# Slots of three tile pools made 32 bytes longer, and two raw weight buffers in place of three, in a two-layer float32 decoder trunk

## The chip, the core and the metric

The kernel runs on one core of a Trainium2 chip. The metric is the device time of one execution in microseconds (us); lower is better. The engines are TensorE (PE: matrix products, with its weight loads shown apart as PEld), VectorE (DVE), ScalarE (ACT), GpSimd (POOL) and SyncE (SP, which here issues most DMA transfers). SBUF is the on-chip memory of 128 partitions; an address below is a byte offset within a partition, which is the same for all 128.

## The reference

A trunk of two layers over 1024 tokens with a width of 1024, in float32. Layer 0 mixes tokens with latent attention (8 heads), layer 1 with a gated spatial unit in chunks of 128 tokens. Each mixer is followed by a feed-forward block of width 4096 and by a gated per-layer embedding of width 256.

```python
def reference(x, p, positions, norm_mix, norm_ffn, norm_ple, ...):
    h = x
    for i in range(2):
        hn = rms_norm(h, norm_mix[i])
        h = h + (mla_mixer(hn, ...) if i % 2 == 0 else gmlp_mixer(hn, ...))
        hn = rms_norm(h, norm_ffn[i])
        h = h + jnp.square(jax.nn.relu(hn @ ffn_w_up[i])) @ ffn_w_down[i]
        hn = rms_norm(h, norm_ple[i])
        h = h + jax.nn.sigmoid(hn @ ple_w_gate[i]) * (p[i] @ ple_w_proj[i])
    return h

def gmlp_mixer(hn, w_in, ln_g, ln_b, w_s, b_s, w_out):
    u, v = jnp.split(jax.nn.gelu(hn @ w_in), 2, axis=-1)
    v = layer_norm(v, ln_g, ln_b)           # then in chunks of 128 tokens, 8 groups
    sv = jnp.einsum('gts,bnsgd->bntgd', w_s * mask, v) + b_s.T
    return (u * sv) @ w_out
```

## The kernel before

**Products.** Every operand of a product is split into a high and a low part (`split`, L106: ACT copies to the 4-byte type fp32r, DVE subtracts), and a product is three matmuls: high by high, high by low, low by high. A matmul has a stationary operand of 128x128, which its own weight load brings in, and a moving operand of mostly 512 columns. In `gemm` (L134) weights stand still and activations move; in the first product of the gated unit (`proj_mm`, tiles vp and up) it is the other way round. The output is feature-major: 128 rows by 1024 tokens in two chunks of 512.

**Pools.** The tile framework cuts SBUF into pools, each a row of equal slots that its tiles take in turn; a tile waits until the last reader of the slot's former tile is done. Those of the change:

- pa, tag a: 2 slots of 16 KB: hidden activations of the feed-forward (f_ah, f_al), the gated unit's y (yh, yl), heads 4 to 7 of the attention output (o4h, o4l), latents, gates (sig).
- pw, tag w: 6 slots of 4 KB: split weights (wh, wl, wb).
- phn, tag hn: 32 slots of 2 KB: the normed residual (n_00h, n_00l, and so on: feature tile, chunk, high or low part), and before that the attention output of heads 0 to 3 (oh, ol).
- pr, tag raw: 3 slots of 4 KB: unsplit weights (raw), x in layer 0's start (x), p (praw), parked values (vr).

All slot lengths are multiples of 512 bytes, so that all slots of a pool stand at one address modulo 512. In the built program this is 288 for the w and a slots and 320 for the hn slots.

**What is where.** Feed-forward up products (tiles f0u, f1u): moving hn (320), stationary w (288). Down products (f0d, f1d): moving a (288), stationary w (288). Output products: go moves a against w; wo moves hn in its first half, a in its second, against w. pg (the embedding's gate) moves hn against w. vp and up move weights (288) against stationary hn slices (320).

**Order.** `ffn` (L253) runs 8 slices s of 512 hidden features: up products, squared ReLU into f_ah and f_al, down products added to the residual h. Weight blocks of 512 KB are loaded by SP as slots come free (L114), so SP runs ahead by as many blocks as pr has slots. After the up products of slice 1, `p_split` (L311) loads p in two halves into raw slots, turns them with PE transposes (tile pp) and splits them into pth and ptl; then come the down products of slice 1. The last slice's down products go one token chunk at a time (`down_sweeps`, L294, tile names wb). Sums of squares for the norm are products with a tile of ones (onesr, L214). In layer 0's start `block_x` transposes one block of 128 tokens of x (tiles x, xp) at a time. The identity for transposes, idf, is made by POOL at the very start (L71). The order on each engine is set by a scheduler from the code's order and its own estimates.

Of the kernel before, what the change touches and what calls it, by code (L numbers as in the profile page):

```python
# [8 lines left out]
F32 = mybir.dt.float32  # L9
# [7 lines left out]
P = 128  # L17
T = 1024
# [21 lines left out]
def trunk(ctx: ExitStack, tc: tile.TileContext, I, out):  # L40
# [6 lines left out]
    pw = ctx.enter_context(tc.tile_pool(name="pw", bufs=6))  # L47
    pr = ctx.enter_context(tc.tile_pool(name="pr", bufs=3))
    pt = ctx.enter_context(tc.tile_pool(name="pt", bufs=4))
# [18 lines left out]

# [1 line left out]
    idf = const.tile([P, P], F32, name="idf")  # L70
# [28 lines left out]
    def gain(kind, layer):  # L99
        o = kind * 16 + layer * 8  # L100
        return [gT[:, o + k:o + k + 1] for k in range(KT)]

# [1 line left out]
    cnt = [0]  # L104
# [15 lines left out]
    def load_packed(w, k0, f0, nk, nf):  # L120
        """a block whose hi and lo share one slot"""
        cnt[0] += 1
        i = cnt[0]
        raw = pr.tile([P, nk, nf], F32, tag="raw", name=f"raw{i}")
        nc.sync.dma_start(raw, w[k0 * P:(k0 + nk) * P, f0:f0 + nf].rearrange("(k p) f -> p k f", p=P))
        both = pw.tile([P, 2, nk, nf], F32R, tag="w", name=f"wb{i}")
        split(both[:, 0], both[:, 1], raw)
        return both[:, 0], both[:, 1]

# [1 line left out]
    par = [0]  # L131
    CS = [slice(0, 512), slice(512, T)]

    def gemm(blocks, rhs, f, name, seq=False, only=None):  # L134
        """one 128-row output tile, over both token chunks or one; rhs[k][c] = (hi, lo).
        Returns (accumulator, columns) units."""
        if only is not None:
            acc = {only: pso(name)}
            units = [(acc[only], CS[only])]
            csets = [(only,)]  # L140
        else:
            par[0] ^= 1
            if par[0]:
                full = psg(name)
                acc = [full[:, CS[c]] for c in range(2)]
                units = [(full, slice(0, T))] if not seq else [(acc[c], CS[c]) for c in range(2)]
            else:
                acc = [pso(f"{name}_{c}") for c in range(2)]
                units = [(acc[c], CS[c]) for c in range(2)]
            csets = [(0,), (1,)] if seq else [(0, 1)]  # L150
        nk = len(rhs)
        w = [(hi[:, kk, f * P:(f + 1) * P], lo[:, kk, f * P:(f + 1) * P]) for hi, lo in blocks for kk in range(hi.shape[1])]
        for cset in csets:
            for k, (wh, wl) in enumerate(w):
                for c in cset:
                    mm(acc[c], wh, rhs[k][c][0], k == 0, False)
                for c in cset:
                    mm(acc[c], wh, rhs[k][c][1], False, False)
                for c in cset:
                    mm(acc[c], wl, rhs[k][c][0], False, k == nk - 1)  # L160
        return units
# [3 lines left out]

# [1 line left out]
    class Norm:  # L167
        """split of h * gain per (feature tile, token chunk); the scale per token is applied after the product"""

# [39 lines left out]
        def sums(self, c, st):  # L209
            """sum of squares of chunk c on every partition of st, an accumulator of 512 columns"""  # L210
            if c not in self.shl:
                self.halve(c)
            shl = self.shl[c]
            mm(st, onesr, shl[:, 0], True, False)  # L214
            mm(st, onesr, shl[:, 1], False, True)
            self.st[c] = st

        def roots(self, *chunks):
            """1/rms on every partition"""
            if self.rb is None:  # L220
                self.rb = pb.tile([P, T], F32, tag="rb", name=f"{self.name}_rb")
            with tc.issue_after(self.last.ins):
                table = S.preload_act_table_set(LNEXP)
            for c in chunks:
                rb, st = self.rb[:, CS[c]], self.st[c]
                with tc.issue_after(table.ins):
                    S.activation(rb, st, AF.Ln, bias=epst, scale=1.0 / D)
                vr = tmp(f"{self.name}{c}_vr", [P, 2, 512])
                v, rr = vr[:, 0], vr[:, 1]
                S.activation(v, st, AF.Identity, bias=epst, scale=1.0 / D)  # L230
                S.activation(rb, rb, AF.Exp, scale=-0.5)
                S.activation(rr, rb, AF.Square)
                V.scalar_tensor_tensor(v, v, -0.5, rr, op0=ALU.mult, op1=ALU.mult)
                V.scalar_tensor_tensor(rb, v, 1.5, rb, op0=ALU.add, op1=ALU.mult)
# [5 lines left out]
        def tokens(self, c, pp=None):  # L240
            """the scale per token, tokens on partitions"""
            if self.r is None:
                self.r = pb.tile([P, NB], F32, tag="rtok", name=f"{self.name}_r")
            if pp is None:
                pp = pso(f"{self.name}_tok{c}")
            for b in range(4):
                PE.transpose(pp[:, b * P:(b + 1) * P], self.rb[:, (c * 4 + b) * P:(c * 4 + b + 1) * P], idf)
            V.tensor_copy(self.r[:, c * 4:c * 4 + 4], pp.rearrange("p (b q) -> p b q", q=P)[:, :, 0])

# [1 line left out]
    halves = {}  # L251
# [42 lines left out]
    def down_sweeps(w, k0, rhs, h, name, nxt, late):  # L294
        """one token chunk after the other, so that the next product can start on the first"""
        for c in range(2):
# [12 lines left out]

# [1 line left out]
    def p_split(i):  # L311
        """p transposed and split: two k tiles of [128, T]"""
        pth = pb.tile([P, 2, T], F32R, tag="pth", name=f"pth{i}")
# [46 lines left out]

# [1 line left out]
    def load_cols(w, f0, name, slots):  # L362
        """columns of a [1024, F] weight as moving operand: per k tile (hi, lo), in the order of use"""
        nf = 256 if slots == "w" else 512
# [19 lines left out]
    def gmlp(h, nrm, nxt):  # L384
# [12 lines left out]
        def spatial_weights():  # L397
            # masked spatial weights, transposed and split; bias per position
            wr = pr.tile([P, 8, P], F32, tag="raw", name="wsraw")
# [30 lines left out]
        for cc, (_, f0, nf) in enumerate(plan):  # L430
# [28 lines left out]
            w = nw  # L459
# [3 lines left out]

        # layer norm statistics
        mv = const.tile([P, NB, 2], F32, name="mv")
# [64 lines left out]

# [1 line left out]
    def ple_out(i, h, nrm):  # L532
# [61 lines left out]

# [1 line left out]
    def mla(h, park):  # L596
        w_down, w_uq, w_ukv, w_out = (I[n][0] for n in ("mla_w_down", "mla_w_uq", "mla_w_ukv", "mla_w_out"))
        with tc.tile_pool(name="pm", bufs=1) as pm:
# [12 lines left out]
            def small_loads():  # L611
                """what the rotary tables and the later norms take"""
                pi = pm.tile([NB, P], I32, name="posi")
# [10 lines left out]
                return gb, pi, gq, inv  # L624
            # down projection weights, gains folded in
            xraw = {}
# [126 lines left out]
            def drain(*gens):  # L753
                """lets each generator run, the later ones three steps behind"""
                live = list(gens)
                n = 0
                while live:
                    for j, g in list(enumerate(gens)):
                        if g in live and n >= 3 * j and next(g, True):
                            live.remove(g)  # L760
                    n += 1
# [3 lines left out]
            def rotary_key(hf):  # L765
                """shared rotary key of half of the tokens: [hi; lo] stacked on partitions"""
                hb = slice(hf * 4, hf * 4 + 4)
# [17 lines left out]

            # per head
            kT, vt, qt, prob, O, proj, pts = ({} for _ in range(7))
# [7 lines left out]
            def q_weights(hp, part):  # L795
                """query weights of a pair of heads: k tiles 0 and 1, or 2"""
                n = 384
# [288 lines left out]
    def rsqrt_small(ss, eps, name):  # L1086
        """1/sqrt(ss + eps) on a small tile, one Newton step after the tables"""
        n = ss.shape[1]
# [10 lines left out]
    def wo_first(rhs, h):  # L1099
        """first half of the output projection, a step per next()"""  # L1100
        w = I["mla_w_out"][0]
# [9 lines left out]
    for _ in filler:  # L1111
        pass
    phn = ctx.enter_context(tc.tile_pool(name="phn", bufs=32))
    n1 = Norm("n1", gain(1, 0))
    rhs1 = []
# [49 lines left out]
```

## Time and profile before

| | before |
|---|---|
| times of the runs | 2746.99 and 2745.89 us, median 2746.44 |
| span of the profiled execution | 2745.7 us |
| TensorE busy | 2711.9 us (99%), 13600 matmuls |
| weight loads busy | 2285.2 us (83%), 13600 |
| VectorE, ScalarE, GpSimd busy | 45%, 33%, 12% |
| DMA traffic | 163.54 MB, mean 60 GB/s |

The profile is of one execution. Its own time is known by its span alone, from the first to the last instruction; the two timed runs lie 0.2 and 1.3 us above that span, which is what may lie around it. Matmuls overlap in a pipeline, so the duration of one (some 390 ns) is no price; the price is the distance from one start to the next, called the pitch below.

### The profile page before, as it was taken

Reading aid. Unit: us, or ns where it says so; the run is one execution under the profiler, and the core shown is the slowest. Engines: PE = TensorE matmul, PEld = TensorE weight load, DVE = VectorE, ACT = ScalarE, POOL = GpSimd, SP = SyncE. Lnnn points to the kernel's source line nnn. Section 1 sums busy time; section 2 is a strip of 40 time slices with the busy share of each in tenths; the row PEclk is TensorE's granted clock in tenths of the full one; section 3 lists DMA queues with packets and bytes.
Section 4 is the critical chain, followed back from the end, with each engine's and each line's share of the span. In section 5 each row is a group of like instructions: output and inputs, shape, how many; then the busy total and the mean of one; then the engine's idle time right before and its main releaser. Section 6 shows DMA issues by size and latency. Waiting matters only on the chain.

```text
span 2745.7 us, 33465 instructions
## 1 busy us (share of the span) xinstructions
PE 2711.9 (99%) x13600; PEld 2285.2 (83%) x13600; DVE 1230.3 (45%) x1964; ACT 905.3 (33%) x1815; POOL 318.9 (12%) x459
## 2 busy tenths in 40 slices
PE   8999999999999999999999999999999999999999
PEld 8999888888888888887888788888888888888899
DVE  5777774533333333375522534436433333333652
ACT  4677772411221122164422312215221122211541
POOL 4444330000000000001211332120000000000000
PEclk9999999999999999999999999999999999999999
DMA  5100012112111111132332312211121111111221
GB/s 164 54 18 6 23 55 69 47 47 65 50 46 47 46 53 48 34 99 75 100 104 94 94 40 84 85 46 54 49 65 40 51 49 47 54 46 39 68 90 35
DMA packets 151209, 163.54 MB, mean 60 GB/s; under 512 B 6496, under 2 KB 133024, under 8 KB 151056
## 3 DMA queue, kind: packets, MB, share of 16 engines
q1 hardware_dynamic: 146240, 146.31, 17.0%
q0 software_dynamic: 4816, 15.10, 1.8%
q8 instruction: 107, 1.75, 0.3%
q14 instruction: 46, 0.38, 0.0%
HBM read 144.61 MB, written 16.78 MB: 59 GB/s over the span
## 4 chain that ended last, share of the span: by engine, by line
PE 87%; DVE 4%; ACT 3%; issue 1%; DMA 0%; POOL 0%; DVEq 0%; ACTq 0%; POOLq 0%
PE f0u L64 13%; PE f1u L64 13%; PE f1d L64 13%; PE f0d L64 13%; PE vp L64 6%; PE up L64 6%; PE go L64 6%; PE e L64 4%; PE wo L64 3%; PE pg L64 3%; PE s L64 2%; PE pq L64 1%; PE av L64 1%; PE pk L64 1%; PE sv L64 1%
## 5 line engine op out<-in xcount | busy, mean ns | idle before, releaser
L107 ACT CAST wh<-raw 128x1024 fp32r<-128x1024 f32 x160 | 168.8, 1055 | 783.5 <-PE f0d L64 258.8
L108 DVE TENSOR_TENSOR wl<-raw,wh 128x1024 fp32r<-128x1024 f32 x160 | 195.0, 1219 | 68.3 <-ACT wh L107 59.4
L289 DVE TENSOR_TENSOR h<-f0d,h 128x512 f32<-128x512 f32 (+1 forms) x84 | 70.4, 866 | 192.1 <-PE f0d L64 192.1
L289 DVE TENSOR_TENSOR h<-f1d,h 128x512 f32<-128x512 f32 (+1 forms) x84 | 70.4, 866 | 192.0 <-PE f1d L64 192.0
L64 PE MATMUL f1d<-f_ah,wh 128*128 128x512 f32 x448 | 138.1, 389 | 0.0
L64 PE MATMUL f0d<-f_ah,wh 128*128 128x512 f32 x448 | 138.1, 389 | 0.0
L64 PE MATMUL f1d<-f_al,wh 128*128 128x512 f32 x448 | 138.0, 389 | 0.0
L64 PE MATMUL f0d<-f_al,wh 128*128 128x512 f32 x448 | 138.0, 389 | 0.0
L64 PE MATMUL f0d<-f_ah,wl 128*128 128x512 f32 x448 | 138.0, 389 | 0.0
L64 PE MATMUL f1d<-f_ah,wl 128*128 128x512 f32 x448 | 137.9, 389 | 0.0
L346 POOL TENSOR_TENSOR h<-sig,h 128x512 f32<-128x512 f32 x16 | 21.9, 1388 | 896.5 <-DVE sig L345 885.2
L271 DVE SCALAR_TENSOR_TENSOR f1t<-f1u,n_rb 128x512 f32<-128x512 f32 (+1 forms) x48 | 40.2, 866 | 177.2 <-PE f1u L64 177.1
L271 DVE SCALAR_TENSOR_TENSOR f0t<-f0u,n_rb 128x512 f32<-128x512 f32 (+1 forms) x48 | 40.2, 866 | 177.0 <-PE f0u L64 176.9
L64 PEld LDWEIGHTS f1d<-f_al,wh 128*128 128x128 f32 x448 | 84.1, 188 | 17.6
L64 PEld LDWEIGHTS f0d<-f_al,wh 128*128 128x128 f32 x448 | 84.1, 188 | 17.6
L64 PEld LDWEIGHTS f0d<-f_ah,wl 128*128 128x128 f32 x448 | 84.1, 188 | 17.6
L64 PEld LDWEIGHTS f1d<-f_ah,wl 128*128 128x128 f32 x448 | 84.1, 188 | 17.6
L64 PEld LDWEIGHTS f0d<-f_ah,wh 128*128 128x128 f32 x448 | 84.0, 188 | 17.5
L64 PEld LDWEIGHTS f1d<-f_ah,wh 128*128 128x128 f32 x448 | 84.0, 188 | 17.5
L272 ACT ACTIVATE f1t<-f1t 128x512 f32<-128x512 f32 (+1 forms) x48 | 36.9, 774 | 160.2 <-DVE f1t L271 160.2
L272 ACT ACTIVATE f0t<-f0t 128x512 f32<-128x512 f32 (+1 forms) x48 | 36.8, 774 | 159.9 <-DVE f0t L271 159.9
L64 PE MATMUL go<-yh,wh 128*128 128x512 f32 x256 | 84.1, 393 | 1.9 <-ACT yh L107 1.9
(2173 smaller groups left out, 7240.6 us busy)
## 6 DMA issues: line engine op xcount, KB each, us to landing
raw<-in_ffn_w_up_dram SPq DMA_DIRECT2D x64, 512.0 KB, 3.7
raw<-in_ffn_w_down_dram SPq DMA_DIRECT2D x56, 512.0 KB, 3.4
raw<-in_ffn_w_down_dram SPq DMA_DIRECT2D x32, 256.0 KB, 2.9
raw<-in_ple_w_gate_dram SPq DMA_DIRECT2D x16, 512.0 KB, 3.8
vr<-vpark SPq DMA_DIRECT2D x16, 512.0 KB, 3.7
raw<-in_gmlp_w_out_dram SPq DMA_DIRECT2D x16, 512.0 KB, 3.4
vpark<-vg POOLq DMA_DIRECT2D x24, 256.0 KB, 2.3
x<-in_x_dram SPq DMA_DIRECT2D x8, 512.0 KB, 3.8
```

What stands on the lines that cost most here:

```text
L64: PE.matmul(o, l, r, start=start, stop=stop)
L107: S.copy(hi, src)
L108: V.tensor_tensor(lo, src, f32(hi), op=ALU.subtract)
L271: V.scalar_tensor_tensor(t[:, c], u, 0.0, rb[:, c], op0=ALU.max, op1=ALU.mult)
L272: S.activation(t[:, c], t[:, c], AF.Square)
L289: V.tensor_tensor(h[j][:, c], u, h[j][:, c], op=ALU.add)
L346: G.tensor_tensor(h[j][:, cs], sg, h[j][:, cs], op=ALU.add)
```

## The change

1. A function `stagger` allocates one tile with 8 float32 elements (32 bytes) more than the pool's tiles have, which makes every slot of that tag 32 bytes longer, and fills it with zeros on POOL (so that it is written at all). It is called for w and a at the very start, ahead of the identity, and for hn after phn is opened. Nothing reads these tiles.
2. The addresses follow. In the built program the w slots stand at 352, 384, 416, 448, 480 and 0 modulo 512, the a slots at 288 and 320, and the 32 hn slots at all 16 multiples of 32, each twice.
3. pr has 2 slots in place of 3.

```diff
-    pr = ctx.enter_context(tc.tile_pool(name="pr", bufs=3))
+    pr = ctx.enter_context(tc.tile_pool(name="pr", bufs=2))
...
+    def stagger(pool, tag, n):
+
+        G.memset(pool.tile([P, n + 8], F32, tag=tag, name=f"stagger_{tag}"), 0.0)
+
+    stagger(pw, "w", 1024)
+    stagger(pa, "a", 4 * T)
+
...
     phn = ctx.enter_context(tc.tile_pool(name="phn", bufs=32))
+    stagger(phn, "hn", 512)
     n1 = Norm("n1", gain(1, 0))
```

The rest of the diff removes comments. Lines of the kernel after stand 7 or 8 further down.

On POOL the start of the program, before and then after (idf is the identity, maskf the causal mask, posi the positions):

```order
L1151 MEMSET const-uint8-127 128x1
L1161 UNCONDITIONAL_BRANCH
masks.py:197 MEMSET idf 128x128
L605 MEMSET maskf 128x128
masks.py:199 ISA
masks.py:199 AFFINE_SELECT idf<-idf 128x128
```

```order
L1159 MEMSET const-uint8-127 128x1
L1169 UNCONDITIONAL_BRANCH
L71 MEMSET stagger_w 128x1032
L71 MEMSET stagger_a 128x4104
masks.py:197 MEMSET idf 128x128
L612 MEMSET maskf 128x128
masks.py:199 ISA
masks.py:199 AFFINE_SELECT idf<-idf 128x128
```

The two new fills stand ahead of the identity.

On SP the loads around `p_split` of layer 0, before and then after, with the semaphores that each waits for (DVE: the subtraction that read the slot's former block; PE: the transposes that read praw; DMAHW: an earlier transfer):

```order
L114 DMA raw_6787<-in_ffn_w_up_dram 128x4x256 [waits DMAHW1_49,DVE_49]
L317 DMA praw_6908<-in_p_dram 128x4x256 [waits DMAHW2_49,DVE_49]
L317 DMA praw_6924<-in_p_dram 128x4x256 [waits DMAHW3_49,DVE_49]
L114 DMA raw_6940<-in_ffn_w_down_dram 128x4x256 [waits DMAHW4_49,DVE_49]
L114 DMA raw_7000<-in_ffn_w_down_dram 128x4x256 [waits DMAHW7_49,DVE_49]
L114 DMA raw_7060<-in_ffn_w_down_dram 128x4x256 [waits DMAHW0_49,DVE_49]
L114 DMA raw_7120<-in_ffn_w_down_dram 128x4x256 [waits DMAHW5_49,PE_49]
```

```order
L121 DMA raw_6793<-in_ffn_w_up_dram 128x4x256 [waits DMAHW2_49,DVE_49]
L324 DMA praw_6914<-in_p_dram 128x4x256 [waits DMAHW3_49,DVE_49]
L324 DMA praw_6930<-in_p_dram 128x4x256 [waits DMAHW4_49,DVE_49]
L121 DMA raw_6946<-in_ffn_w_down_dram 128x4x256 [waits DMAHW5_49,PE_49]
L121 DMA raw_7006<-in_ffn_w_down_dram 128x4x256 [waits DMAHW6_49,PE_49]
L121 DMA raw_7066<-in_ffn_w_down_dram 128x4x256 [waits DMAHW7_49,DVE_49]
L121 DMA raw_7126<-in_ffn_w_down_dram 128x4x256 [waits DMAHW0_49,DVE_49]
```

The order is the same; the waits for PE have moved from the fourth down block to the first two.

On ACT around the same place, before and then after (f0t is the hidden tile, pth the high part of p):

```order
L273 CAST f_ah_6654<-f0t_6842 128x1024
L107 CAST wh_7002<-raw_7000 128x1024
L107 CAST wh_7062<-raw_7060 128x1024
L272 ACTIVATE f0t_6897<-f0t_6897 128x512
L107 CAST pth_6906<-pp_6910 128x512
```

```order
L280 CAST f_ah_6660<-f0t_6848 128x1024
L114 CAST pth_6912<-pp_6916 128x512
L279 ACTIVATE f0t_6903<-f0t_6903 128x512 x2
L280 CAST f_ah_6660<-f0t_6903 128x512 x2
L114 CAST pth_6912<-pp_6923 128x512
L114 CAST pth_6912<-pp_6932 128x512
L114 CAST pth_6912<-pp_6939 128x512
L114 CAST wh_6948<-raw_6946 128x1024
L114 CAST wh_7008<-raw_7006 128x1024
```

The casts of the first down blocks have moved behind all four casts of p.

## Rows read from the trace of the kernel before

**Rows 1.** The page: busy time, share and count of each engine; the granted clock of TensorE in 40 slices; the chain that ended last.

```profile
PE 2711.9 (99%) x13600; PEld 2285.2 (83%) x13600; DVE 1230.3 (45%) x1964; ACT 905.3 (33%) x1815; POOL 318.9 (12%) x459
...
PEclk9999999999999999999999999999999999999999
...
PE 87%; DVE 4%; ACT 3%; issue 1%; DMA 0%; POOL 0%; DVEq 0%; ACTq 0%; POOLq 0%
PE f0u L64 13%; PE f1u L64 13%; PE f1d L64 13%; PE f0d L64 13%; PE vp L64 6%; PE up L64 6%; PE go L64 6%; PE e L64 4%; PE wo L64 3%; PE pg L64 3%; PE s L64 2%; PE pq L64 1%; PE av L64 1%; PE pk L64 1%; PE sv L64 1%
```

**Rows 2.** The timeline of PE in a stretch of down products: start, duration, and x2 where two matmuls in a row share a line. The seven lines from the first to the last shown hold two matmuls each, so 12 pitches lie between their starts.

```profile
564.59 0.61 PE L64 MATMUL f0d<-f_ah,wh 128*128 128x512 f32 x2
...
567.31 0.61 PE L64 MATMUL f0d<-f_ah,wh 128*128 128x512 f32 x2
```

**Rows 3.** The timeline of PE in a stretch of up products: the first and the last start of 28 in a row (27 pitches).

```profile
630.06 0.39 PE L64 MATMUL f0u<-n_30l,wh 128*128 128x512 f32 x1
...
636.36 0.40 PE L64 MATMUL f0u<-n_71h,wl 128*128 128x512 f32 x1
```

**Rows 4.** The timeline of PE in the gated unit's up product, where weights move and hn stands still: the first and the last start of 13 in a row (12 pitches).

```profile
1717.87 0.40 PE L64 MATMUL up<-wu2h,n_70l 128*128 128x512 f32 x1
...
1720.67 0.40 PE L64 MATMUL up<-wu2h,n_30l 128*128 128x512 f32 x1
```

**Rows 5.** Groups of PE by form: count, busy time and mean duration of one in ns. The wo product has both pairings in one code.

```profile
L64 PE MATMUL f0d<-f_ah,wh 128*128 128x512 f32 x448 | 138.1, 389 | 0.0
L64 PE MATMUL go<-yh,wl 128*128 128x512 f32 x256 | 82.8, 389 | 0.0
L64 PE MATMUL wo<-oh,wl 128*128 128x512 f32 x64 | 20.1, 395 | 0.0
L64 PE MATMUL wo<-o4h,wl 128*128 128x512 f32 x64 | 19.7, 389 | 0.0
L64 PE MATMUL f0u<-n_11h,wh 128*128 128x512 f32 x32 | 12.7, 397 | 0.0
```

**Rows 6.** Sums over the whole span of the instructions of one tile each: PE, PEld and other busy time with counts, mean clock, DMA share, GB/s. In this order: f0d, f0u, go, wo, up, vp, pg.

```profile
0.00:2746.00 2746.00, 350.18 (x1536) 288.05 (x1536) 81.34 (x100) 1.00 0.19 60
0.00:2746.00 2746.00, 359.89 (x1536) 287.91 (x1536) 40.22 (x48) 1.00 0.19 60
0.00:2746.00 2746.00, 180.28 (x768) 142.70 (x768) 40.47 (x52) 1.00 0.19 60
0.00:2746.00 2746.00, 89.00 (x384) 71.88 (x384) 20.20 (x24) 1.00 0.19 60
0.00:2746.00 2746.00, 183.46 (x768) 142.51 (x768) 22.04 (x32) 1.00 0.19 60
0.00:2746.00 2746.00, 181.08 (x960) 154.16 (x960) 23.91 (x40) 1.00 0.19 60
0.00:2746.00 2746.00, 91.15 (x384) 71.91 (x384) 10.90 (x16) 1.00 0.19 60
```

**Rows 7.** The timeline of PE in a down sweep just behind two products with onesr (address 128 modulo 512): 12 starts from 1201.84 to 1204.37.

```profile
1201.38 0.62 PE L64 MATMUL f0d7st<-n_shl,onesr 128*128 128x512 f32 x2
1201.84 0.40 PE L64 MATMUL f0d<-f_ah,wb 128*128 128x512 f32 x1
1202.07 0.40 PE L64 MATMUL f0d<-f_al,wb 128*128 128x512 f32 x1
1202.31 0.62 PE L64 MATMUL f0d<-f_ah,wb 128*128 128x512 f32 x2
...
1204.37 0.39 PE L64 MATMUL f0d<-f_ah,wb 128*128 128x512 f32 x1
```

**Rows 8.** The timeline of all engines at `p_split` of layer 0.

```profile
636.44 1.06 ACT L107 CAST wh<-raw 128x1024 fp32r<-128x1024 f32 x1 [4.67 <-DMA raw<-in_ffn_w_down_dram]
636.60 1.96 PE L321 MATMUL pp<-idf,praw 128*128 128x128 f32 x16
638.31 0.71 PE L64 MATMUL f0d<-f_ah,wh 128*128 128x512 f32 x2
```

**Rows 9.** The page: split of a weight block, and DMA issues with the median time from issue to landing.

```profile
L107 ACT CAST wh<-raw 128x1024 fp32r<-128x1024 f32 x160 | 168.8, 1055 | 783.5 <-PE f0d L64 258.8
L108 DVE TENSOR_TENSOR wl<-raw,wh 128x1024 fp32r<-128x1024 f32 x160 | 195.0, 1219 | 68.3 <-ACT wh L107 59.4
...
raw<-in_ffn_w_down_dram SPq DMA_DIRECT2D x56, 512.0 KB, 3.4
raw<-in_ffn_w_down_dram SPq DMA_DIRECT2D x32, 256.0 KB, 2.9
...
x<-in_x_dram SPq DMA_DIRECT2D x8, 512.0 KB, 3.8
```

**Rows 10.** The list of PE's waits (total, times, longest in us): the longest one.

```profile
PE cp L745 <- ACT lats L730: 3.2, 1, 3.2
```

**Rows 11.** Two windows, one with that wait and the one behind it: busy time of PE, PEld, DVE, ACT and POOL with counts, granted clock, DMA share, GB/s.

```profile
31.00:36.00 5.00, 1.80 (x13) 1.59 (x12) 4.39 (x10) 2.87 (x13) 2.93 (x2) 0.85 0.55 175
36.00:60.00 24.00, 24.00 (x151) 23.67 (x150) 13.48 (x32) 9.55 (x34) 12.30 (x11) 0.96 0.34 100
```

**Rows 12.** The timeline of the start: fills on POOL, and PE's first work.

```profile
0.31 0.10 POOL L1151 MEMSET const-float32-0.0<- 128x1 f32 x1 [0.31 <-issue]
0.81 0.20 POOL masks.py:197 MEMSET idf<- 128x128 f32 x1 [0.29 <-POOLq L1151]
1.20 0.32 POOL masks.py:199 TENSOR_SCALAR_AFFINE_SELECT idf<-idf 128x128 f32<-128x128 f32 x1
2.66 0.26 PE L94 MATMUL gps<-idf,grawa 16*128 16x16 f32 x1 [2.66 <-DMA grawa<-in_norm_mix_dram]
5.22 1.97 PE L682 MATMUL xp<-idf,x 128*128 128x128 f32 x8 [2.30 <-DMA x<-in_x_dram]
```

**Rows 13.** The timeline of SP and PE: issues of the loads of two blocks of x, and the transposes of one of them; ahead of it, from the answer on the tile x, all 64 transposes of its 8 blocks with the first and the last start.

```profile
L682 PE MATMUL xp<-idf,x x64: 270/273/473, 5.2 to 82.9; 128*128 128x128 f32 x64
...
59.31 5.58 SPq L630 DMA_DIRECT2D x<-in_x_dram  x2
...
72.76 0.71 PE L682 MATMUL xp<-idf,x 128*128 128x128 f32 x5
```

## Prediction, written before the changed kernel ran

> **What bounds the kernel now.** I began with the page. TensorE is busy 99% of the span and 87% of the chain that ended last is its matmuls, at a full granted clock [rows 1]. Almost nothing waits, so two things can move the time: the distance from one matmul's start to the next (the pitch), and new holes in PE's stream. The durations of single matmuls overlap, so I went to the timeline for the pitch. In the down products there are 12 pitches from 564.59 to 567.31, 2.72 us, so 226.7 ns each [rows 2]. In the up products 27 pitches take 636.36 - 630.06 = 6.30 us, 233.3 ns each [rows 3]. In the gated unit's up product 12 pitches take 2.80 us, again 233.3 ns [rows 4]. All three stream 512 columns, at 2.4 GHz 213.3 ns, with a weight load under each. What differs is the addresses: moving and stationary both at 288 in the first case, at 320 and 288 in the other two, whichever of the two is the one that moves. The output product of the attention has both pairings within one code: 389 ns for a single matmul with the heads in pa (288), 395 with those in phn (320), and go and f0d (288) lie at 389, f0u (320) at 397 [rows 5]. I take the address pair as the cause of the two pitches. This is an inference: pool and tile layout change together with the address.
>
> **The pitch after the change.** These are the matmuls with 512 columns by class [rows 6]. Equal addresses: the down products, 2 x 1536; go 768; half of wo, 192; together 4032 at 226.7. Addresses 32 apart: the up products, 2 x 1536; up 768; vp 576 of its 960 (the rest have 256 columns); pg 384; half of wo, 192; together 4992 at 233.3. Their mean is 230.4 ns over 9024 matmuls. Everything else (short products, scores, transposes) I leave where it is.
>
> After the change every pair is drawn from six residues of w, two of a and sixteen of hn. No stretch keeps one pair for more than a few matmuls, and most pairs are unequal. So the down products lose their good pitch, and the up products meet pairs never seen here. The trace has one place where equal-address matmuls run out of step: behind two products with onesr, which stands 160 below, the down sweep makes 11 pitches from 1201.84 to 1204.37, 2.53 us or 230.0 each, before it is back in step [rows 7]. That is the nearest row for a mixture; the bounds are the two pitches of rows 2 and 3. I take 231, nearer to the out-of-step row than to the worse pitch. Down, go and wo then lose 4032 x 4.3 ns = 17.3 us, up, vp, pg and wo gain 4992 x 2.3 ns = 11.5 us: **+6 us**. At 226.7 for all it would be -4992 x 6.6 ns = -33 us, at 233.3 for all +4032 x 6.6 ns = +27 us.
>
> **The third raw slot.** Before, the first down block of slice 1 had a slot of its own beside the two halves of p. Its cast ran from 636.44, under the transposes pp (16 in 1.96 us from 636.60), and the down products began at 638.31 with no idle time [rows 8]. Now both slots hold p, and SP's load of that block waits for the transposes of the first half; all later loads queue behind it on SP. Half of the transposes end at 636.60 + 0.98 = 637.58. The transfer lands 3.4 us later, at 640.98, and the cast takes 1.06: 642.04 [rows 9]. The first down matmul moves from 638.31 to there: 3.7 us. DVE makes the low part in 1.22 us, while PE has four matmuls on the high part, 4 x 0.227 = 0.91: 0.3 us more. The wait on ACT behind the four casts of p costs nothing, as these end within 2 us and the landing is later. So 4.0 us of idle PE in each of the two layers.
>
> Such a hole may cost clock as well. The trace has one of nearly that length: PE waited 3.2 us [rows 10], and the granted clock was 0.85 in the window with it and 0.96 in the 24 us behind [rows 11]. That is 0.15 x 5 + 0.04 x 24 = 1.7 us of full-clock time, part of it inside the hole; I take 1.5 for each layer. Sum 2 x (4.0 + 1.5) = **+11 us**; 8 without the clock, 13 with a landing somewhat late.
>
> In the rest of the feed-forward the third slot is not missed. A block serves 48 matmuls, 11 us, against 3.4 + 1.06 + 1.22 = 5.7 us to bring and split one [rows 9]. In the sweeps a half-size block serves 12 matmuls, 2.7 us; with two slots a block has 5.4 us for 2.9 of transfer and about half of a full split, 1.1: covered by 1.4 us, and if that cover went, each of 32 blocks would cost what it is late. I put **+1 us** (0 to 4) for these, the gated unit's loads through the same slots included.
>
> **The start.** Two fills on POOL stand ahead of the identity. A fill of one column took 0.10 us and one of 128 columns 0.20 [rows 12], so 0.8 ns a column: 1032 columns 0.9 us, 4104 columns 3.3. The identity is done at 5.7 in place of 1.5. The gains' transposition (2.66) waits for it, and so do the first transposes of x, which started at 5.22 when x had landed; they move to about 6.0. POOL's small loads behind it come 4.2 us later and have their first readers much later. **+1 us**, 0 to 5. The fill for hn is on POOL, which is 12% busy: nothing, and 0.5 us if something waited.
>
> **Blocks of x.** With two slots a load of x waits for the block two before it, not three. The block transposed at 72.76 was loaded at 59.31; blocks come every (82.9 - 5.2) / 7 = 11 us, and a load one block later would land at 59.3 + 11.1 + 3.8 = 74.2 [rows 9, 13], 1.4 us late; other blocks have more room. **+1 us**, 0 to 4.
>
> **Sum** on the profiled span of 2745.7, which lies 0.7 below the median of the two runs: 6 + 11 + 1 + 1 + 1 = 20, so 2745.7 + 20 + 0.7 = 2766 us.
>
> **The rivals.**
>
> *A, slower: the mixture is worse than both pitches.* If a start that follows a change of pair falls at 0.24 us, as the one from 1202.07 to 1202.31 did [rows 7], and the varying pairs hold it near there, say at 237, the down side loses 4032 x 10.3 = 42 us and the up side 4992 x 3.7 = 18. With the 14 us of the other terms that is 2746 + 74 = 2820. It turns to slower by 2% (55 us) once the pitches rise by 41 us / 9024 = 4.5 ns, from a mean of 230.4 to 235. For it: residues never paired before, up to 256 bytes apart, come up in the hn products. Against it: even the mean behind the onesr disturbance was 230.0.
>
> *B, faster: the extra over 213.3 ns is a collision that equal strides cause and varying ones avoid.* Half of the extra gone is 9024 x 8.5 ns = 77 us: 2746 - 77 + 14 = 2683, 2.3% faster. It takes a mean pitch of 222.8 or less to pass 2%. Against it: each unequal pair of the trace is slower than the equal one, and nothing with 512 columns runs under 226.7. For it: weight loads are read beside every moving stream (83% busy) [rows 1], so that an address can matter at all. The Trainium skill, page "TensorE: Matmul & The Clock Gate", section "Wait — 56ns, not 53.3ns?", gives a back-to-back pitch of 215.7 ns for 512 columns, which no stretch here reaches; taken as the floor it would make this rival's full gain 9024 x 14.7 = 133 us and the time 2627.
>
> *C, addresses are not the cause.* The two pitches may belong to the pools or tile layouts. Then they stay, and the time is 2746 + 14 = 2760. Against it: the pitch goes with the pair even when moving and stationary change roles [rows 3, 4]. The Trainium skill, page "SBUF — State Buffer", section "Who interferes with whom", gives TensorE one port for the moving operand and an independent one for weight loads, with no term for addresses; by that rule this rival would be the result, and the 6.6 ns between rows 2 and rows 3 speak against it.
>
> *D, all pairs fall into the good pitch:* -33 + 14, so 2727. Seen only where nothing varied.
>
> **How the numbers follow.** 2% of 2746 is 55 us, about what a measurement of this kernel tells from no change. Chances: forecast, pitch term from 0 to +27, 0.5; C 0.1; D and what lies between it and the forecast 0.16; B 0.12; A 0.12. The point is the forecast's, 2766. Forecast, C and D lie within 2%, 0.76. The range reaches down to D, 2727, and up to 233.3 for all with the upper bounds of the other terms: 2746 + 27 + 13 + 4 + 5 + 4 = 2799.
>
> **What would show it.** The down products' pitch read from the timeline should rise from 226.7 to about 231 and the up products' fall from 233.3 to about 231, with no lasting step in either; a hole of 4 us should stand between pp and the first down matmul of slice 1 in both layers, ended by the cast wh, with a dip of the clock behind it; the first xp should start near 6.0. I am wrong if the pitch of the up products falls under 226 (B) or the down products' rises over 235 (A).

## The result, and the profile after

The changed kernel takes 2777.85 us (2775.23 to 2780.47) against 2746.44: a ratio of 1.011, with a 95% interval of 1.0081 to 1.014. It is 31 us slower; 2766 was forecast, in a range of 2727 to 2799. The profiled execution's span grew from 2745.7 to 2778.8 us, by 33.1.

The page of the changed kernel (engines, and the largest down group with the idle time ahead of it) answers to [rows 1, 5]:

```profile
PE 2732.1 (98%) x13600; PEld 2290.4 (82%) x13600; DVE 1230.5 (44%) x1964; ACT 905.3 (33%) x1815; POOL 324.0 (12%) x462
...
L64 PE MATMUL f0d<-f_ah,wh 128*128 128x512 f32 x448 | 141.8, 398 | 3.8 <-ACT wh L114 3.8
```

TensorE has the same 13600 matmuls and 20.2 us more busy time; 398 ns for a single down matmul stands against 389. The rest of the 33.1 us, 12.9, is idle time, and the line shows where one hole lies: 3.8 us in front of a down matmul, until ACT had cast its weight. The sums per tile over the whole span, in the order f0d, f0u, go, wo, up, vp, pg, answer to [rows 6]:

```profile
0.00:2779.00 2779.00, 361.70 (x1536) 290.31 (x1536) 81.37 (x100) 0.99 0.19 59
0.00:2779.00 2779.00, 357.75 (x1536) 288.42 (x1536) 40.22 (x48) 0.99 0.19 59
0.00:2779.00 2779.00, 183.29 (x768) 142.69 (x768) 40.44 (x52) 0.99 0.19 59
0.00:2779.00 2779.00, 89.88 (x384) 71.95 (x384) 20.20 (x24) 0.99 0.19 59
0.00:2779.00 2779.00, 182.28 (x768) 142.44 (x768) 22.06 (x32) 0.99 0.19 59
0.00:2779.00 2779.00, 180.49 (x960) 153.80 (x960) 23.92 (x40) 0.99 0.19 59
0.00:2779.00 2779.00, 90.58 (x384) 72.03 (x384) 10.91 (x16) 0.99 0.19 59
```

The first busy time of each line, that of PE, tells it: f0d 350.18 to 361.70 (some of it behind a hole, at the lower clock), f0u 359.89 to 357.75. The products that had the good pitch lost it, those with the bad one gained a little. The timeline gives the pitch itself. In a stretch of down products 48 pitches take 581.59 - 570.42 = 11.17 us, 232.7 ns each (226.7 in [rows 2]):

```profile
570.42 0.63 PE L64 MATMUL f0d<-f_ah,wh 128*128 128x512 f32 x2
...
581.59 0.63 PE L64 MATMUL f0d<-f_ah,wh 128*128 128x512 f32 x2
```

In a stretch of up products 32 pitches take 641.29 - 633.85 = 7.44 us, 232.5 each (233.3 in [rows 3]):

```profile
633.85 0.40 PE L64 MATMUL f0u<-n_21l,wh 128*128 128x512 f32 x1
...
641.29 0.40 PE L64 MATMUL f0u<-n_71h,wl 128*128 128x512 f32 x1
```

Averaged over all starts of the trace (pitches across a hole or at the lower clock left out), the 512-column products run thus, in ns:

| product | count | before | after | change in all, us |
|---|---|---|---|---|
| down (f0d, f1d) | 3072 | 226.95 | 232.51 | +17.1 |
| go | 768 | 227.30 | 232.49 | +4.0 |
| wo | 384 | 230.28 | 232.59 | +0.9 |
| up of the feed-forward (f0u, f1u) | 3072 | 233.35 | 232.00 | -4.1 |
| up of the gated unit | 768 | 232.99 | 231.47 | -1.2 |
| vp | 576 | 233.34 | 232.15 | -0.7 |
| pg | 384 | 233.39 | 231.91 | -0.6 |

That is +15.4 us. The list of TensorE's waits shows the rest (total, times, longest, in us):

```profile
PE gps L101 <- POOL idf masks.py:199: 6.0, 1, 6.0
PE gps L101 <- DMA grawb<-in_mla_k_nope_g_dram: 4.0, 1, 4.0
PE f0d L64 <- ACT wh L114: 3.8, 1, 3.8
PE f1d L64 <- ACT wh L114: 3.8, 1, 3.8
PE e L64 <- ACT ewp L114: 3.8, 1, 3.8
```

The first is at the start, where the fills delay the identity (before, TensorE waited 2.7 us there for a load). The second is dealt with below, under the fills. The third and fourth are the holes at `p_split`. The timeline around that of layer 0, the answer to [rows 8]:

```profile
641.53 1.96 PE L328 MATMUL pp<-idf,praw 128*128 128x128 f32 x16
...
642.60 1.29 SPq L121 DMA_DIRECT2D raw<-in_ffn_w_down_dram  x2
...
646.16 1.07 ACT L114 CAST wh<-raw 128x1024 fp32r<-128x1024 f32 x1
...
647.28 1.22 PE L64 MATMUL f0d<-f_ah,wh 128*128 128x512 f32 x2 [3.80 <-ACT wh L114]
```

The load starts in the middle of the transposes, lands some 3.5 us later, the cast takes 1.07, and TensorE has been idle 3.80 us. A window around this hole and one around the third shows the clock (the third number from the end):

```profile
640.00:660.00 20.00, 16.20 (x67) 12.95 (x66) 9.88 (x12) 7.16 (x11) 0.00 (x0) 0.83 0.42 131
2630.00:2650.00 20.00, 16.23 (x59) 12.62 (x58) 14.30 (x23) 11.34 (x19) 0.00 (x0) 0.83 0.29 86
```

The third hole, which the prediction didn't have, lies in the last sweep of layer 1. A product e of the output stage stands right behind the sums with onesr and waits for its weight:

```profile
2632.49 0.63 PE L64 MATMUL f1d7st<-n_shl,onesr 128*128 128x512 f32 x2
2636.89 1.31 PE L64 MATMUL e<-ewp,pth 128*128 128x256 f32 x3 [3.77 <-ACT ewp L114]
...
2639.06 1.05 PE L64 MATMUL f1d<-f_ah,wb 128*128 128x512 f32 x2
2639.91 0.63 PE L64 MATMUL f1d<-f_al,wb 128*128 128x512 f32 x1
2640.34 1.05 PE L64 MATMUL f1d<-f_ah,wb 128*128 128x512 f32 x2
```

Three matmuls take 2640.34 - 2639.06 = 1.28 us, 427 ns each: 512 columns at 1.2 GHz, the lower level of the clock. TensorE had been idle for 3.77 us before. In the kernel before, the same product came 24 down matmuls later and waited for nothing:

```profile
2606.35 0.62 PE L64 MATMUL f1d7st<-n_shl,onesr 128*128 128x512 f32 x2
...
2612.29 0.59 PE L64 MATMUL e<-ewp,pth 128*128 128x256 f32 x3
```

Where the 33.1 us came from, read off the first start of the same product in both traces, each from the start of its span:

| stretch | later by, us | of it pitch, us | the rest, us |
|---|---|---|---|
| up to the first up product of layer 0 | 4.3 | 0.9 (wo) | 3.4, start and blocks of x |
| up products of slice 1 to those of slice 2, layer 0 | 7.7 | 0.8 | 6.9, hole and clock |
| the same, layer 1 | 6.6 | 0.8 | 5.8, hole and clock |
| from the last down slice of layer 0 to layer 1's feed-forward | -2.6 | 2.6 | -5.2, waits gone in the gated unit |
| last down slice of layer 1 to the end | 7.5 | 1.1 | 6.4, hole and clock |
| all the rest | 9.5 | 9.2 | 0.3 |

### The profile page after: what moved, and what is told of

It reads as the page before. It is cut to its first block, busy times and chain, and to the rows that moved or that the text cites. A ratio compares the mean times of both kernels' runs of the same rounds, so it can differ in the third digit from the quotient of the medians.

```text
span 2778.8 us, 33456 instructions
## 1 busy us (share of the span) xinstructions
PE 2732.1 (98%) x13600; PEld 2290.4 (82%) x13600; DVE 1230.5 (44%) x1964; ACT 905.3 (33%) x1815; POOL 324.0 (12%) x462
## 4 chain that ended last, share of the span: by engine, by line
PE 88%; DVE 3%; ACT 3%; issue 1%; POOL 0%; DMA 0%; DVEq 0%; ACTq 0%; POOLq 0%
PE f0d L64 13%; PE f1d L64 13%; PE f1u L64 13%; PE f0u L64 13%; PE up L64 6%; PE go L64 6%; PE vp L64 6%; PE e L64 4%; PE wo L64 3%; PE pg L64 3%; PE s L64 2%; PE pq L64 1%; PE av L64 1%; PE pk L64 1%; PE pj L64 1%
## 5 line engine op out<-in xcount | busy, mean ns | idle before, releaser
L64 PE MATMUL go<-yl,wh 128*128 128x512 f32 x256 | 84.8, 397 | 0.0
```

The lines of the kernel that those rows point to most:

```text
L64: PE.matmul(o, l, r, start=start, stop=stop)
```

## The experiments

Theory: the pitch of a product with 512 columns is set by the addresses of its moving and its stationary operand modulo 512, and the two raw slots make holes; the two effects add up. The rivals are C of the prediction (pools and tile layouts, not addresses), and holes that come of the longer slots' new order. The ratios below are to runs of the kernel before made together with these, median 2747.13 us.

**Two raw slots alone.**

```diff
-    pr = ctx.enter_context(tc.tile_pool(name="pr", bufs=3))
+    pr = ctx.enter_context(tc.tile_pool(name="pr", bufs=2))
```

> The kernel before with two raw slots and nothing else. Theory (the pitch and the raw slots add up independently): the pitches stay at 226.9 ns (down products) and 233.4 (up products), and the holes of the changed kernel come alone: 3.8 us of idle PE in front of the first down matmul of slice 1 in each layer, with about 3 us of lost clock behind each, and the one of 3.8 us in the last sweep, so 2746 + 18 = 2764 us, less whatever waits vanish in the gated unit (5 us): 2759 to 2764. Rival (the holes come of the scheduler's new order under the longer slots): about 2746, no hole at pp.

Measured 2759.61 us, ratio 1.0045 (1.0029 to 1.0061). The down products ran at 226.95 ns and the up products at 233.35, as before. Its list of waits has the three holes:

```profile
PE e L64 <- ACT ewp L107: 4.4, 1, 4.4
PE f1d L64 <- ACT wh L107: 3.8, 1, 3.8
PE f0d L64 <- ACT wh L107: 3.8, 1, 3.8
```

Against the kernel before, layer 0 lost 5.7 us at `p_split`, layer 1 lost 6.6, the end 6.8 and the start 1.0; the gated unit won 5.9. That last one is a matter of order: with two slots the scheduler interleaves the products go, yp and sv otherwise. The waits of TensorE from 1190 to 1930 us, in the kernel before:

```profile
PE yp L516 <- DVE u L510: 2.0, 4, 0.5
PE go L64 <- ACT yh L107: 1.9, 3, 0.8
PE sv L64 <- DVE vhl L108: 1.4, 1, 1.4
PE pg L64 <- DVE sig L335: 0.6, 1, 0.6
PE gtok L247 <- DVE n_rb L234: 0.3, 1, 0.3
```

With two raw slots the same window lists only the last two. So the raw slots alone make some 13 of the 31 us, and the holes don't need the longer slots. The traces settle the rival further: TensorE's 13600 matmuls stand in the same order, by tile names and shapes, in this kernel and in the changed one except at the start, among the first 122. Against the kernel before, both differ in the gated unit and in the last sweep alone; at `p_split` the order is the old one, and the holes there come of the late loads.

**All operands at one address.** One tile of 480 bytes ahead of phn puts hn at 288, where w and a stand; three raw slots.

```diff
+    pad = ctx.enter_context(tc.tile_pool(name="pad", bufs=1))
+    V.memset(pad.tile([P, 120], F32, name="pad"), 0.0)
     phn = ctx.enter_context(tc.tile_pool(name="phn", bufs=32))
```

> The kernel before with one tile of 480 bytes ahead of the pool phn, so that its slots stand at 288 modulo 512 like those of w and a; three raw slots, no longer slots. Theory (the address pair sets the pitch): up products, pg, vp, up and the first half of wo fall from 233.4 to 227 ns, 4992 x 6.4 ns = 32 us, so 2714 us. Rival C of the prediction (pools or tile layouts set it): pitch and time unchanged, 2746.

Measured 2717.22 us, ratio 0.9887 (0.9871 to 0.9903): 30 us faster than before. In the timeline of its up products 29 pitches take 626.53 - 619.96 = 6.57 us, 226.6 ns each:

```profile
619.96 0.39 PE L64 MATMUL f0u<-n_00h,wl 128*128 128x512 f32 x1
...
626.53 0.39 PE L64 MATMUL f0u<-n_51l,wh 128*128 128x512 f32 x1
```

Its sums for f0d and f0u have become equal (349.99 and 349.63 us):

```profile
0.00:2746.00 2746.00, 349.99 (x1536) 288.07 (x1536) 81.30 (x100) 1.00 0.19 60
0.00:2746.00 2746.00, 349.63 (x1536) 288.31 (x1536) 40.20 (x48) 1.00 0.19 60
```

pg ran at 226.8, vp at 226.8, up at 227.6. Pools and tiles are the same, one fill of the new tile has been added, and all 13600 matmuls stand in the order of the kernel before; only the address has moved. Rival C falls, and the two pitches of the kernel before were a matter of addresses.

**Longer slots for hn alone**, three raw slots.

```diff
     phn = ctx.enter_context(tc.tile_pool(name="phn", bufs=32))
+    V.memset(phn.tile([P, 512 + 8], F32, tag="hn", name="stagger_hn"), 0.0)
```

> The kernel before with longer slots for hn alone, three raw slots. Theory (the address pair; a mixture runs at 232 whatever its parts): the down products and go stay at 227, up products, pg, vp and up go from 233.4 to 232, 4992 x 1.4 ns = 7 us, so 2739. Rival (a varying residue of one operand spoils the other products too, by the state it leaves): down products above 230 and a time of 2750 or more.

Measured 2741.99 us, ratio 0.998 (0.997 to 0.999); 2739 was expected, and 2750 or more by the rival. The down products stayed at 227.05 and go at 227.13; up products went to 232.27, vp to 232.52. The stepping addresses of one pool change only the products that read it, and this mixture is a little better than a fixed distance of 32.

**Streams of matmuls alone.** No trunk; two tiles with moving and stationary operands at chosen addresses.

```python
def run(mo, wo, count, tag):          # mo, wo: bytes beyond a multiple of 512
    for i in range(count):
        m = mo(i) // 4 + 512 * (i % 4)
        w = wo(i) // 4 + 128 * ((i // 2) % 8)
        PE.matmul(o, W[:, w:w + 128], M[:, m:m + 512], ...)
```

> No trunk, and its output is not the reference's (it copies x out): streams of matmuls of 512 moving columns, each with a weight load, 48 for each distance between the moving and the stationary address modulo 512 (0 to 480 in steps of 32, with the stationary at two places 32 bytes apart; also 4, 8, 16 and 24), then streams in which the moving, the stationary or both addresses step by 32 from one matmul to the next. Theory: 226.7 ns at distance 0, 233.3 at 32 and 480, values of 231 to 234 elsewhere, about 232 where one address steps, and 226.7 where both step together. Rival (what counts is an absolute alignment, not the distance): equal distances give different pitches at the two places.

The groups of the trace for distance 0, 32 and 256 and for the last, equal stream (mean duration of one in ns behind the busy time):

```profile
L36 PE MATMUL end<-M,W 128*128 128x512 f32 x96 | 22.0, 389 | 0.0
...
L36 PE MATMUL d32a<-M,W 128*128 128x512 f32 x48 | 11.4, 395 | 0.0
...
L36 PE MATMUL d256a<-M,W 128*128 128x512 f32 x48 | 11.1, 390 | 0.0
L36 PE MATMUL d0a<-M,W 128*128 128x512 f32 x48 | 11.1, 389 | 0.0
```

Pitch in the second half of each stream, in ns, with the stationary operand at two places 32 bytes apart (the mean of 23 pitches, the one into the next stream left out):

| distance, bytes | 0 | 32 | 64 | 96 | 128 | 160 | 192 | 224 |
|---|---|---|---|---|---|---|---|---|
| first place | 226.7 | 233.3 | 233.3 | 233.4 | 233.1 | 234.3 | 233.3 | 233.3 |
| second place | 226.7 | 233.3 | 229.0 | 233.1 | 232.7 | 234.6 | 233.4 | 233.3 |
| distance + 256, first place | 226.7 | 233.3 | 233.3 | 233.4 | 233.2 | 234.3 | 233.2 | 233.3 |

Distances 256 apart have one pitch: the pattern repeats every 256 bytes, not every 512. No stream runs below 226.7. The two places agree within 0.4 ns except at 64, so the rival of an absolute alignment has that one case for it. Distances of 4, 8, 16 and 24 bytes gave 236.8, 233.3, 231.5 and 233.5. With one or both addresses stepping the pitch was 234.1 to 234.2. About 232 had been expected for one and 226.7 for both together, and both were wrong. No other engine works beside these streams, so the two pitches of the trunk need no other engine.

**Which pair counts.**

> Streams alone again, no trunk; the output is x copied out. In the first three the moving and the stationary address both step by 32 bytes from one matmul to the next: with the stationary one matmul behind, in step, and one ahead. Theory (the pair that counts is the moving operand of a matmul with the stationary operand of the next, which is loaded under it): one behind gives distance 0 in every such pair and 226.7 ns, in step 234 as measured, one ahead 233 to 235. Rival (stepping itself spoils the pitch): about 234 in all three. Then seven fixed pairs of moving and stationary address, four times each, behind a short matmul of 128, 168, 208 or 248 columns. Theory (a pair has one pitch of its own): equal pitches for a pair in all four, 226.7 for the two equal pairs. Rival (the pitch is a state left by what ran before): a pair has two or more pitches.

The stationary one matmul behind ran at 230.7, in step at 227.5, one ahead at 230.9. So the theory of the expectation falls (it wanted 226.7, 234 and more), and so does its rival. The stream in step had run at 234.2 in the run before this: it has at least two states. Among the fixed pairs the equal ones came to 226.7 behind every one of the four short matmuls, within 3 to 11 matmuls, and distance 32 to between 233.2 and 233.5 in all four. Distance 64 ran at 228.9 in all eight cases, the first place of the streams above included, which had 233.3 there: so it wasn't the place. Distance 128 had 232.3 in five cases and 233.6 to 233.7 in three. A fixed pair thus has a pitch of its own at distance 0 and 32, and two of them at 64 and 128, by what ran before. Why a pair has the pitch that it has is open.

**The holes filled.** The changed kernel, with p and the last embedding's small weight in slots of pt.

```diff
-            raw = pr.tile([P, 4, 256], F32, tag="raw", name=f"praw{i}{hf}")
+            raw = tmp(f"praw{i}{hf}", [P, 4, 256])
...
-            raw = pr.tile([P, 2, 256], F32, tag="raw", name=f"ewpr{q}")
+            raw = tmp(f"ewpr{q}", [P, 2, 256])
```

> The changed kernel with p and the last embedding's small weight loaded into slots of the pool pt (tag t) in place of raw slots. Theory (three holes come of the two raw slots: 7 and 6 us with the lost clock at pp of the two layers, 7 at the first product e of the last sweep): 2777.9 - 20 = 2758 us, pitches as in the changed kernel (232). Rival (the holes only move, since something else of two slots is late): 2770 or more.

Measured 2760.07 us, ratio 1.0045 (1.003 to 1.006), with down and up products at 232.53 and 232.00 as in the changed kernel. The three waits are gone (the longest left at f0d, f1d or e is 0.9 us); a window from before the transposes of p to behind them has no idle time and the full clock:

```profile
636.00:656.00 20.00, 20.00 (x96) 16.39 (x95) 10.14 (x14) 6.57 (x10) 0.00 (x0) 1.00 0.32 105
```

The three stretches with the holes are together 18 us shorter than in the changed kernel. This is not the holes alone: the scheduler wrote another order at `p_split` and in the last sweep, and the start came 1.8 us earlier too. What is left over the kernel before, 13 us, is the pitch (15.4), the start and the won waits.

**Fills of one column**, the changed kernel otherwise.

```diff
-        G.memset(pool.tile([P, n + 8], F32, tag=tag, name=f"stagger_{tag}"), 0.0)
+        G.memset(pool.tile([P, n + 8], F32, tag=tag, name=f"stagger_{tag}")[:, :1], 0.0)
```

> The changed kernel with fills of one column in place of whole tiles, all addresses the same. Theory (the fills ahead of the identity and of POOL's first loads make the start late; up products of layer 0 begin 4.2 us later than before, against 0.8 with two raw slots alone): 3.4 us less, 2774.5. Rival (the loads of x through two slots make it late): unchanged, 2778.

Measured 2776.99 us (2774.88 to 2777.58), which the times alone don't tell from the changed kernel's 2777.85. The traces do: its span is 2775.9 against 2778.8, and the up products of layer 0 begin 1.5 us later than before in place of 4.3. The fills cost 2.8 us of it, so the loads of x, the rival, make the smaller part. Their rows in the trace of the changed kernel, and the transposition that waited for POOL's loads behind them:

```profile
0.80 0.96 POOL L71 MEMSET stagger_w<- 128x1032 f32 x1 [0.29 <-POOLq L1159]
...
1.70 3.60 POOL L71 MEMSET stagger_a<- 128x4104 f32 x1
...
20.12 0.29 PE L101 MATMUL gps<-idf,grawb 34*128 34x34 f32 x1 [3.98 <-DMA grawb<-in_mla_k_nope_g_dram]
```

The same transposition in the kernel before:

```profile
26.65 0.25 PE L94 MATMUL gps<-idf,grawb 34*128 34x34 f32 x1
```

There, and with fills of one column, 90 matmuls stand ahead of it and it waits for no load. In the changed kernel the scheduler has put it behind 34, while its loads are issued from 9.0 us on in place of 4.6.

**hn 256 bytes from the rest.** The kernel before with a tile of 224 bytes ahead of phn in place of 480.

> The kernel before with one tile of 224 bytes ahead of phn: hn at 32 modulo 512, w and a at 288, so 256 apart. Theory (the pitch repeats every 256 bytes, as in the streams alone, where distances 0 and 256 both gave 227): like the aligned kernel, up products at 227 and 2717 us. Rival (inside the program it is equality modulo 512): up products at 231 or more, 2740 to 2750.

Measured 2716.64 us, ratio 0.9889 (0.9874 to 0.9904), up products at 226.67. In the program too the pitch repeats every 256 bytes.

**Aligned, with two raw slots and no raw slot for p.** The aligned kernel with two raw slots, and p and the small weight in slots of pt.

> The aligned kernel with two raw slots, and p and the last embedding's small weight in slots of pt. Theory (with two raw slots the gated unit lost 5.9 us of waits, and the holes are avoided here): 2717 - 5.9 + 0.8 = 2712 us. Rival (the order that gave this came with the holes or costs elsewhere): 2717 or more.

Measured 2713.07 us, ratio 0.9876 (0.9862 to 0.9891). The span was 2710.7 against 2711.7 for the aligned kernel with three raw slots, so whether the two raw slots add something to the alignment isn't settled; the intervals overlap. The two traces, one execution each, show where the 5.9 us may have gone: against the aligned kernel the gated unit's stretch is 5.2 us shorter, but the start is 2.5 us longer and the last sweep with the output 1.7.

## Why the prediction was right or wrong

**The direction and the likeliest case were right, and the time was 12 us over the forecast.** The address pair sets the pitch, the down products lose what the up products only partly gain, the holes at `p_split` appear: each has been shown apart (the aligned kernel, hn alone, two raw slots alone). Rivals A (235 and more), B (222.8 and less) and D (226.7 for all) didn't come: all 512-column products ran between 231.5 and 232.6. C was refuted by the aligned kernel. The effects add up: by spans the raw slots alone make 14.2 us, the pitch 15.4 and the fills 2.8, together 32.4 of the 33.1.

**The pitch term was mis-sized:** +6 forecast, +15.4 measured. The step at fault is the choice of 231, from the 230.0 behind the products with onesr [rows 7]. That stretch was a return to the good pitch, as the streams show: equal pairs come back within 11 matmuls. Of its 11 pitches the first eight average 231.5 and the last three 226.7, so its mean was no sample of a mixture. Measured was a mean of 232.2 over the 9024 matmuls; the 1.2 ns more than 231 are 11 us. Why the mixture comes to 232 isn't shown: most fixed distances run at 233 to 234, and the streams with stepping addresses ran at 227.5 to 234.2.

**The holes at p_split were right:** 4.0 us of idle time forecast, 3.80 measured, and with the clock 5.5 forecast against 6.9 and 5.8 (5.7 and 6.6 with two raw slots alone). Together 12.7 against 11: the path, the landing and the dip of the clock were as forecast.

**The rest of the raw slots was wrong twice, in opposite directions.** The prediction asked only whether loads land in time in the order that stands, and put +1 for it. But two slots change the order that the scheduler writes: a product e moved ahead of 24 down matmuls in the last sweep and waited 3.77 us for its weight, 6.4 us with the clock; in the gated unit waits of 5.2 us vanished. The two nearly cancel to the forecast +1, which is luck.

**The start** came to 3.4 us with the blocks of x, against 2 forecast. The fills took 0.96 and 3.60 us (0.9 and 3.3 forecast), and the first xp started at 6.18 (near 6.0 forecast). What failed is that POOL's small loads "have their first readers much later". That holds for the order before; in the new order a transposition of gains stands 56 matmuls earlier and waits 4.0 us for the last of these loads. The fills make 2.8 us, against 1 forecast. The blocks of x cost 1.0 with two raw slots alone, as forecast.

## What to carry to other kernels

When a product streams without holes, compare the start-to-start pitch of its forms before anything else; where two forms differ by a few ns, look at the addresses of moving and stationary operand. Here they are best equal modulo 256: 224 bytes of padding in one place gave 30 us, while spreading the addresses brought every product to 231.5 to 232.6 ns, near the worse of the two pitches. The streams show the good pitch for pairs that stay the same; two addresses that step together ran at 234.2 in one of two runs. A buffer fewer, or a longer fill, is priced by the order that it makes the scheduler write, not by its loads alone: so compare the order of TensorE's matmuls as well. A hole of 3.8 us on TensorE cost another 2 to 3 in clock.

## What the runs showed of the hardware

- Matmuls of 512 columns of the type fp32r with a weight load each ran at 226.7 ns in streams of one address pair where moving and stationary address are equal modulo 256, at 233.3 where they are 32 apart, and at 229 to 237 at the other distances tried; none averaged the 213.3 ns of the columns alone.
- Products of 256 columns hardly care, and the other way round: the 256-column matmuls of vp ran at 118.3 ns with the operands 32 apart (kernel before) and at 119.8 with equal addresses (aligned kernel).
- A stream whose addresses step together ran at 227.5 in one run and 234.2 in another; why it has two states is open.
- At each idle time of 3.8 us the granted clock fell to 1.2 GHz (427 ns for 512 columns): in layer 0 towards its end (a granted clock of 0.88 from 645 to 647 us, 0.50 from 648 to 653), in layer 1 a microsecond into the work behind it (1.00 from 2062 to 2063, 0.53 in the next). The pitch of 427 ns ended 6.1 and 4.5 us after the work had begun. Each such hole cost 2 to 3 us beyond its idle time.
